# Four pairs of k-tiles instead of three by seven products in the FFNs of a decoder block, with a smaller descriptor ring and shared tiles

## The chip, the cores and the metric

The kernel runs on one core of a Trainium2 chip. The metric is the device time of one execution in microseconds (us); lower is better. Engines are named as in the profile: PE multiplies matrices, PEld loads its weights, DVE and ACT are the vector and scalar engines, POOL is GpSimd (it issues one kind of DMA here), SP issues nearly all other DMAs. A weight element is fp32 and is used as a rounded high half and a low half (the rest), both in a narrower fp32 type that PE takes.

## The reference, cut to what matters

One decoder block over 256 rows of width 2048, all in fp32:

```python
h = h + 0.5 * swiglu(rms_norm(h, ffn1_norm), ffn1_w_gu, ffn1_w_down)     # FFN1
h = h + hybrid_mixer(rms_norm(h, mix_norm), ...)                         # mixer
h = h + 0.5 * swiglu(rms_norm(h, ffn2_norm), ffn2_w_gu, ffn2_w_down)     # FFN2
gate = sigmoid(rms_norm(h, ple_norm) @ ple_w_gate)                       # last stage
h = h + gate * (p @ ple_w_proj)
out = rms_norm(h, final_norm)

def swiglu(x, w_gu, w_down):
    gate, up = split(x @ w_gu, 2)        # w_gu 2048 x 11264, w_down 5632 x 2048
    return (silu(gate) * up) @ w_down
```

## The kernel before, in words

**Products.** The weights stream from HBM in pairs of k-tiles (a tile is 128 rows; a pair is 128x1024 numbers, 512 KB, tile `raw`). ACT rounds a pair to `whi` (L70), DVE takes the rest `wlo` (L71), and PE does three matmuls for each product of 128x128 by 128x512: high by high, high by low, low by high. The next weights are asked for two ahead (`LEAD`); `raw` has four buffers, `whi` and `wlo` three. The input is split the same way (`nTh`/`nTl` for the normalised input, `hTh`/`hTl` for silu(gate)*up).

**Groups.** Each FFN is done in 17 groups, in three parts of 3, 4 and 4 gate/up blocks: a "gu" group is one 512-column block of gate and one of up over K = 2048 (eight pairs of k-tiles each), a "dn" group is two 512-column blocks of the down product over the part's K (six or eight pairs). After a part's gu groups come its two dn groups, so the order is gu0 to gu2, dn, dn, gu3 to gu6, dn, dn, gu7 to gu10, dn, dn.

**Seven products.** Of most groups the first `ns` pairs of both blocks don't go by plain products but as a 2x2 block product by seven products (Winograd's form of Strassen's): rows of the input in two halves of 128, columns in the two blocks, K in the two k-tiles of a pair. The weights' four quarters, raw and unsplit, are tiles R00, R01, R10 and R11 of 128 x (ns x 512) elements with one buffer each, loaded by SP (L269). Seven sums S0 to S6 are formed from them by `all_sums`: each is rounded by ACT (`shi`, L282) and its rest taken by DVE (`slo`, L283), two buffers each. R00 is the source of S0, S1, S2 and S5; it changes in between by two additions on DVE (L287), and after S2 by a DMA that adds a quarter read again from HBM (`add_loaded`, L291, issued from POOL). R01 is added to in the same way after S0. Each sum then feeds 3 x ns matmuls (L314 to L316), and at two of the seven ACT copies and DVE adds move partial results between the four PSUM banks (L321, L322). The matching sums of the input are made by the generator `halves`, two pairs at a time: an addition high + low (tile `tT`, L396), four additions and subtractions (tile `S`, L403), the rounding on ACT (`Sh`, L404), the rest on DVE (`Sl`, L405).

**The order of work.** The seven products of a group are carried out during the group ahead of it, between that group's plain pairs. `plan` writes this order: list `at` says after which plain pairs the sevenths stand, `loads` after which of them the R loads of the group after next are asked for. Weights, sums and loads go through one FIFO, `order`, drained by `next_weights`. Behind every plain pair `lanes.step()` advances generators with work on DVE, ACT and SP: lane 0 has a gu group's output (L426: times up, then the 32x32 transposes L165 and two DMAs through DRAM, then the split into `hTh`/`hTl`, L434 and L435) and the norms' transposes, lane 1 has `halves`. A scheduler of the framework then fixes each engine's instruction order. All queues are in order: what stands behind a waiting instruction waits too.

**The other stages.** The mixer between the FFNs is not touched. In the last stage (`fin`), for three column blocks, `embed` multiplies the embeddings p by `w_pp` (one pair), `accumulate` multiplies the normalised h by `w_pg` (eight pairs), and `gated` applies the sigmoid and updates h on DVE (L578 to L586).

Of the kernel before, what the change touches and what calls it, by code (L numbers as in the profile page):

```python
# [10 lines left out]
F32 = mybir.dt.float32  # L11
# [18 lines left out]
NS = 3  # L30
NS_DOWN = tuple(3 if i1 - i0 == 4 else 2 for i0, i1 in PARTS)
# [8 lines left out]
def block_kernel(ctx, tc, a, out):  # L40
# [156 lines left out]
    def norm_block(nT, which, j, tmp):  # L197

        if j < 3:
            lanes.add(0, norm_block_behind(nT, which, j, tmp))  # L200
            return
# [129 lines left out]
    def plan(n):  # L331
# [17 lines left out]
        made = []  # L349
        for i, group in enumerate(groups):  # L350
# [3 lines left out]
            at, loads = [], {}  # L354
            if follower is not None and follower.ns:
                first = 2 if group.ns else 8
                at = [first + j * (n_plain - 1 - first) // 7 for j in range(7)]
                if not group.ns:

                    loads.setdefault(max(at[0] - 5, 0), []).extend(follower.loads())  # L360
                if after is not None and after.ns:
                    for x, one in zip((5, 6, 7, 7), after.loads()):
                        loads.setdefault(at[x] if x < 7 else min(at[6] + 1, n_plain - 1), []).append(one)
# [16 lines left out]
    for nb in range(3):  # L380
        order += [("pair", a["w_pp"][nb])] + [("pair", a["w_pg"][nb][g]) for g in range(KD // 2)]
    order.append(("pair", a["w_pp"][3]))

    def halves(kind, his, los, ns, wait=0):
# [7 lines left out]
        for g0 in range(0, ns, 2):  # L392
# [3 lines left out]
            nc.vector.tensor_tensor(out=x, in0=hi[:, 0:2 * n].bitcast(F32).rearrange("p k x -> p (k x)"),  # L396
                                    in1=lo[:, 0:2 * n].bitcast(F32).rearrange("p k x -> p (k x)"), op=ALU.add)
            x = x.rearrange("p (g j t y) -> p g j t y", g=n, j=2, t=2)
            a11, a12, a21, a22 = (x[:, :, j, t, :] for t in range(2) for j in range(2))
            s = fp.tile([P, 4, 2, P], F32, tag="S", name="S")[:, :, 0:n]  # L400
            for o, y, z, op in ((0, a21, a22, ALU.subtract), (1, s[:, 0], a11, ALU.subtract),
                                (2, a21, a11, ALU.subtract), (3, s[:, 1], a12, ALU.add)):
                nc.vector.tensor_tensor(out=s[:, o], in0=y, in1=z, op=op)  # L403
            nc.scalar.copy(sh[:, :, g0:g0 + n], s)  # L404
            nc.vector.tensor_tensor(out=sl[:, :, g0:g0 + n], in0=s, in1=sh[:, :, g0:g0 + n], op=ALU.subtract)  # L405
            yield
# [9 lines left out]
        sides[kind] = side  # L416

    def ffn(n, nT, r, scale, next_norm, stat):
        xs = picker(*nT)
        late = callable(r)  # L420
        with tc.tile_pool(name="ffn", bufs=1) as fp:
# [24 lines left out]
            for group, todo in ffn_plan[n]:  # L446
# [11 lines left out]
                for kind, one in todo:  # L458
# [19 lines left out]
                    if dn:  # L478
# [7 lines left out]
                        if group.last:  # L486
                            norm_block(nxt, next_norm, nb, lambda: fp.tile([P, 2, 4, P], F32, tag="tT", name="tT"))
                            lanes.advance(0)
# [755 lines left out]
```

## Time and profile before

| what | value |
|---|---|
| median of 3 runs | 1964.15 us (1963.59 to 1965.22) |
| the profiled execution, and its span | 1965.08 us, 1963.4 us |
| granted PE clock, mean | 0.997 |
| busy PE, DVE, ACT (share of the span) | 99%, 78%, 59% |
| FFN1, mixer, FFN2, last stage (us from the span's start) | 0 to 702, 702 to 1165, 1165 to 1854, 1854 to 1963 |
| DMA queues, share of 16 engines' span | hardware 61.9%, software (POOL's) 13.5% |

In a row of instructions the columns are line, engine, operation, out<-in by tile names with shapes, count, then the busy sum in us and the mean of one in ns, and the idle time of the engine just ahead of them with what ended it. A row of waits reads: who waited for whom, us in total, times, the longest. A row of DMA issues has the count, the size of one and the median time from issue to landing. A timeline row is start, length, engine, line, operation, and in brackets how long the engine had been idle and for what.

### The profile page before, as it was taken

What the parts mean: (1) busy time and instruction counts of PE and PEld (TensorE: products, weight loads), DVE (VectorE), ACT (ScalarE), POOL (GpSimd) and SP (SyncE); (2) the same over time, 40 slices, a digit from 0 to 9 for tenths busy, and PEclk for the clock granted to TensorE, in tenths of its full rate; (3) what the DMA queues carried; (4) which work ended last, traced back from release to release, by engine and by line L of the source; (5) the groups of instructions that cost most, each with busy time, mean ns of one, the idle gap of its engine ahead of it and who ended that gap; (6) DMA issues with size and microseconds to landing.
All of it is one profiled execution on the core that took longest, in us unless ns stands there. A gap on an engine that the chain in (4) does not pass through costs nothing. (4 is left out here: it accounts for less than half of the span.)

```text
span 1963.4 us, 24730 instructions
## 1 busy us (share of the span) xinstructions
PE 1943.0 (99%) x8941; PEld 1606.3 (82%) x8941; DVE 1534.3 (78%) x1771; ACT 1151.2 (59%) x1401; POOL 83.3 (4%) x108
## 2 busy tenths in 40 slices
PE   9999999999999999999999999999999999999998
PEld 7887888888888888878878888888888888888887
DVE  6879878887888766794786678888889887798755
ACT  6655655565656557654545456565566555665554
POOL 0000000000000000000100000000000000000000
PEclk9999999999999999999999999999999999999999
DMA  9978887888888764555564788887888878887764
GB/s 298 301 238 253 268 263 244 264 257 247 265 274 242 224 215 159 179 178 195 175 200 149 250 284 245 255 266 248 252 262 265 289 231 242 256 275 243 235 208 146
DMA packets 166554, 468.28 MB, mean 239 GB/s; under 512 B 20640, under 2 KB 59552, under 8 KB 166304
## 3 DMA queue, kind: packets, MB, share of 16 engines
q1 hardware_dynamic: 156352, 418.57, 61.9%
q0 software_dynamic: 8928, 46.67, 13.5%
q10 hardware_dynamic: 1152, 1.47, 0.3%
q8 instruction: 70, 1.15, 0.2%
q14 instruction: 52, 0.43, 0.1%
HBM read 444.62 MB, written 22.02 MB: 238 GB/s over the span
## 5 line engine op out<-in xcount | busy, mean ns | idle before, releaser
L70 ACT CAST whi<-raw 128x1024 fp32r<-128x1024 f32 (+1 forms) x531 | 557.3, 1051 | 535.0 <-PE pj L107 110.9
L71 DVE TENSOR_TENSOR wlo<-raw,whi 128x1024 fp32r<-128x1024 f32 (+1 forms) x531 | 643.8, 1217 | 211.6 <-ACT whi L70 208.2
L283 DVE TENSOR_TENSOR slo<-R,shi 128x1536 fp32r<-128x1536 f32 (+1 forms) x217 | 365.8, 1687 | 129.0 <-ACT shi L282 127.3
L282 ACT CAST shi<-R 128x1536 fp32r<-128x1536 f32 (+1 forms) x217 | 309.7, 1429 | 170.0 <-PE g L316 47.2
L472 PE MATMUL g<-wlo,nTh 128*128 128x512 f32 x476 | 186.8, 392 | 0.5 <-DVE wlo L71 0.5
L471 PE MATMUL g<-whi,nTh 128*128 128x512 f32 x476 | 185.0, 390 | 2.2 <-ACT whi L70 2.2
L473 PE MATMUL g<-whi,nTl 128*128 128x512 f32 x476 | 186.2, 391 | 0.0
L472 PE MATMUL u<-wlo,nTh 128*128 128x512 f32 x476 | 185.3, 389 | 0.0
L471 PE MATMUL u<-whi,nTh 128*128 128x512 f32 x476 | 185.3, 389 | 0.0
L473 PE MATMUL u<-whi,nTl 128*128 128x512 f32 x476 | 185.3, 389 | 0.0
L105 PE MATMUL pj<-whi,nTh 128*128 128x512 f32 x448 | 179.7, 402 | 0.0
L106 PE MATMUL pj<-wlo,nTh 128*128 128x512 f32 x448 | 175.9, 393 | 2.2 <-DVE wlo L71 2.0
L472 PE MATMUL d<-wlo,hTh 128*128 128x512 f32 x448 | 174.6, 390 | 1.0 <-DVE wlo L71 1.0
L107 PE MATMUL pj<-whi,nTl 128*128 128x512 f32 x448 | 175.4, 391 | 0.0
L471 PE MATMUL d<-whi,hTh 128*128 128x512 f32 x448 | 174.5, 389 | 0.0
L473 PE MATMUL d<-whi,hTl 128*128 128x512 f32 x448 | 174.4, 389 | 0.0
L472 PEld LDWEIGHTS g<-wlo,nTh 128*128 128x128 f32 x476 | 89.8, 189 | 21.0 <-DVE wlo L71 2.4
L471 PEld LDWEIGHTS g<-whi,nTh 128*128 128x128 f32 x476 | 89.5, 188 | 21.3 <-ACT whi L70 2.8
L287 DVE TENSOR_TENSOR R<-R 128x1536 f32<-128x1536 f32 (+1 forms) x62 | 104.5, 1686 | 0.9
L473 PEld LDWEIGHTS g<-whi,nTl 128*128 128x128 f32 x476 | 89.8, 189 | 18.5
L473 PEld LDWEIGHTS u<-whi,nTl 128*128 128x128 f32 x476 | 89.4, 188 | 18.6
L471 PEld LDWEIGHTS u<-whi,nTh 128*128 128x128 f32 x476 | 89.4, 188 | 18.5
(304 smaller groups left out, 3221.5 us busy)
## 6 DMA issues: line engine op xcount, KB each, us to landing
raw<-in_w_gu SPq DMA_DIRECT2D x220, 512.0 KB, 5.6
raw<-in_w_down SPq DMA_DIRECT2D x112, 512.0 KB, 5.4
raw<-in_w_in SPq DMA_DIRECT2D x112, 512.0 KB, 3.4
R<-in_w_gu2q SPq DMA_DIRECT2D x40, 768.0 KB, 5.8
R<-in_w_gu1q SPq DMA_DIRECT2D x36, 768.0 KB, 6.1
scr<-tb SPq DMA_DIRECT2D x74, 256.0 KB, 4.8
raw<-in_w_out SPq DMA_DIRECT2D x32, 512.0 KB, 4.6
raw<-in_w_pg SPq DMA_DIRECT2D x32, 512.0 KB, 4.3
```

The costliest lines, as they stand in the source:

```text
L70: nc.scalar.copy(hi[:, j, :], raw[:, j, :])
L71: nc.vector.tensor_tensor(out=lo[:, j, :], in0=raw[:, j, :], in1=hi[:, j, :], op=ALU.subtract)
L105: nc.tensor.matmul(outs[t], xh[:, c], whi[:, j, :], start=st, stop=False)
L106: nc.tensor.matmul(outs[t], xh[:, c], wlo[:, j, :], start=False, stop=False)
L107: nc.tensor.matmul(outs[t], xl[:, c], whi[:, j, :], start=False, stop=sp)
L282: nc.scalar.copy(hi, w)
L283: nc.vector.tensor_tensor(out=lo, in0=w, in1=hi, op=ALU.subtract)
L287: nc.vector.tensor_tensor(out=self.raw[x], in0=self.raw[x], in1=self.raw[y], op=ALU.add)
L471: nc.tensor.matmul(out, xh[:, c], whi[:, j, :], start=st, stop=False, skip_group_check=True)
L472: nc.tensor.matmul(out, xh[:, c], wlo[:, j, :], start=False, stop=False, skip_group_check=True)
L473: nc.tensor.matmul(out, xl[:, c], whi[:, j, :], start=False, stop=sp, skip_group_check=True)
```

## The change

Of the groups that use seven products, all but the four dn groups of the first part and of each FFN's kind with six pairs now do four pairs that way (half of K), not three: 27 of 31 groups. Sums and quarters of these groups are 128x2048 instead of 128x1536 (1 MB instead of 768 KB a load), and two plain pairs per group fall away. `plan` puts the sevenths behind consecutive plain pairs, from the second pair on (from the third, where the follower is of the other kind; from the ninth in a group without sevenths of its own), instead of spreading them; the R loads of the group after next stand at the fifth, sixth and seventh seventh, and the fourth load at the start of the next group (`carried`).

The room for it comes from the ring of DMA descriptors in on-chip memory (`dynamic_dma_scratch_size`, 4096 instead of the default 16384) and from tiles that share a buffer: `S` of `halves` now uses the tag of `sil` (the silu(gate) tile), and half of the norms' transposed blocks do too, on lane 1. The split of the embeddings' input (`ph`, `pl`) stood ahead of FFN2 in a pool of its own; it is now a generator in the last stage, on lane 2. There the embed's pair also comes behind the gate's eight pairs, not ahead of them.

```diff
-NS = 3
-NS_DOWN = tuple(3 if i1 - i0 == 4 else 2 for i0, i1 in PARTS)
+NS = 4
+NS_DOWN = tuple(4 if i1 - i0 == 4 else 2 for i0, i1 in PARTS)
...
-    def norm_block(nT, which, j, tmp):
+    def norm_block(nT, which, j, tmp, lane=0):
 
         if j < 3:
-            lanes.add(0, norm_block_behind(nT, which, j, tmp))
+            lanes.add(lane, norm_block_behind(nT, which, j, tmp))
...
-        made = []
+        made, carried = [], []
...
-            at, loads = [], {}
+            at, loads, carried = [], {0: carried}, []
             if follower is not None and follower.ns:
-                first = 2 if group.ns else 8
-                at = [first + j * (n_plain - 1 - first) // 7 for j in range(7)]
+                first = 8 if not group.ns else 1 if group.kind == follower.kind else 2
+                at = [min(first + j, n_plain - 1) for j in range(7)]
                 if not group.ns:
 
                     loads.setdefault(max(at[0] - 5, 0), []).extend(follower.loads())
                 if after is not None and after.ns:
-                    for x, one in zip((5, 6, 7, 7), after.loads()):
-                        loads.setdefault(at[x] if x < 7 else min(at[6] + 1, n_plain - 1), []).append(one)
+                    *three, last = after.loads()
+                    for x, one in zip((4, 5, 6), three):
+                        loads.setdefault(at[x], []).append(one)
+                    carried = [last]
...
-        order += [("pair", a["w_pp"][nb])] + [("pair", a["w_pg"][nb][g]) for g in range(KD // 2)]
+        order += [("pair", a["w_pg"][nb][g]) for g in range(KD // 2)] + [("pair", a["w_pp"][nb])]
...
-            s = fp.tile([P, 4, 2, P], F32, tag="S", name="S")[:, :, 0:n]
+            s = fp.tile([P, 4, 2, P], F32, tag="sil", name="S")[:, :, 0:n]
...
-                            norm_block(nxt, next_norm, nb, lambda: fp.tile([P, 2, 4, P], F32, tag="tT", name="tT"))
-                            lanes.advance(0)
+                            norm_block(nxt, next_norm, nb, lambda x=("tT", "sil")[nb % 2]:
+                                       fp.tile([P, 2, 4, P], F32, tag=x, name="tT"), nb % 2)
+                            lanes.advance(nb % 2)
...
-    pp = ctx.enter_context(tc.tile_pool(name="pp", bufs=1))
-    pT = act.tile([P, 2, T], F32, tag="nat", name="pT", bufs=4)
-    nc.sync.dma_start(out=pT, in_=a["pT"])
-    ph = pp.tile([P, 2, T], F32R, tag="ph", name="ph")
-    pl = pp.tile([P, 2, T], F32R, tag="pl", name="pl")
-    nc.scalar.copy(ph, pT)
-    nc.vector.tensor_tensor(out=pl, in0=pT, in1=ph, op=ALU.subtract)
...
+        ph = fp.tile([P, 2, T], F32R, tag="ph", name="ph")
+        pl = fp.tile([P, 2, T], F32R, tag="pl", name="pl")
+
+        def split_p():
+            pT = act.tile([P, 2, T], F32, tag="nat", name="pT", bufs=4)
+            nc.sync.dma_start(out=pT, in_=a["pT"])
+            for _ in range(3):
+                yield
+            nc.scalar.copy(ph, pT)
+            nc.vector.tensor_tensor(out=pl, in0=pT, in1=ph, op=ALU.subtract)
+
+        lanes.add(2, split_p())
...
         for nb in range(3):
-            e = embed(nb)
             gt = [mm_ps("gt") for _ in range(2)]
             accumulate(gt, xs, KD)
+            e = embed(nb)
...
-    nc = _bacc.Bacc("TRN2", target_bir_lowering=False, num_devices=1)
+    nc = _bacc.Bacc("TRN2", target_bir_lowering=False, num_devices=1, dynamic_dma_scratch_size=4096)
```

**DVE in the last gu group of the second part.** From the low half of S1 to that of S2 (tiles: `slo` of a sum, `wlo` of a plain pair, `R` an addition to a quarter, `S`, `Sl` and `tT` the halves of the following dn group's input), DVE's order before was:

```order
L283 TENSOR_TENSOR slo<-R,shi 128x1536
L71 TENSOR_TENSOR wlo<-raw,whi 128x1024
L287 TENSOR_TENSOR R<-R 128x1536
L403 TENSOR_TENSOR S<-tT 128x128 x2
L403 TENSOR_TENSOR S<-S,tT 128x128
L71 TENSOR_TENSOR wlo<-raw,whi 128x1024
L403 TENSOR_TENSOR S<-S,tT 128x128
L71 TENSOR_TENSOR wlo<-raw,whi 128x1024
L405 TENSOR_TENSOR Sl<-S,Sh 128x4x128
L283 TENSOR_TENSOR slo<-R,shi 128x1536
```

and in the changed kernel, for the same stretch and the four rows behind it (L409, L416 and L418 are the lines of `halves` now):

```order
L283 TENSOR_TENSOR slo<-R,shi 128x2048
L416 TENSOR_TENSOR S<-S,tT 128x256
L287 TENSOR_TENSOR R<-R 128x2048
L418 TENSOR_TENSOR Sl<-S,Sh 128x4x256
L409 TENSOR_TENSOR tT<-hTh,hTl 128x1024
L71 TENSOR_TENSOR wlo<-raw,whi 128x1024
L416 TENSOR_TENSOR S<-tT 128x256 x2
L416 TENSOR_TENSOR S<-S,tT 128x256
L283 TENSOR_TENSOR slo<-R,shi 128x2048
L416 TENSOR_TENSOR S<-S,tT 128x256
L71 TENSOR_TENSOR wlo<-raw,whi 128x1024 x2
L418 TENSOR_TENSOR Sl<-S,Sh 128x4x256
```

The last part of the first pass of the halves, which stood ahead of this stretch, is in it now, with the addition `tT` of the second; the second pass is twice as wide and its end has moved behind S2.

**ACT in the last stage.** From the weights ahead of the first sigmoid (`sg`, L582, now L590) to those behind it, ACT's order before was:

```order
L70 CAST whi<-raw 128x1024 x5
L582 ACT_TABLE_LOAD
L582 ACTIVATE sg<-gt,rstd_15319 128x512 x2
L70 CAST whi<-raw 128x1024 x2
L218 ACTIVATE junk,stat<-h 128x512 x2
L70 CAST whi<-raw 128x1024 x7
```

and now, with the input's rounding `ph` in it:

```order
L70 CAST whi<-raw 128x1024 x3
L578 CAST ph<-pT 128x512
L70 CAST whi<-raw 128x1024 x4
L590 ACT_TABLE_LOAD
L590 ACTIVATE sg<-gt,rstd_14911 128x512
L70 CAST whi<-raw 128x1024
L590 ACTIVATE sg<-gt,rstd_14911 128x512
L70 CAST whi<-raw 128x1024
L218 ACTIVATE junk,stat<-h 128x512
L70 CAST whi<-raw 128x1024
```

The two sigmoids stood together ahead of the next weights; now a weight pair stands between them.

More of the change, by code (lines that the diff above doesn't have):

```diff
@@ L391, in halves, with side @@
         sl = fp.tile([P, 4, NS, P], F32R, tag="Sl", name="Sl")
+        def side(i, g):
+            if i in (0, 4, 5):
+                k, t = 2 * (g % 2) + (i > 0), i // 5
+                c = slice(t * P, (t + 1) * P)
+                return his[g // 2][:, k, c], los[g // 2][:, k, c]
+            x = {1: 0, 2: 1, 3: 2, 6: 3}[i]
+            return sh[:, x, g, :], sl[:, x, g, :]
+        sides[kind] = side
         for g0 in range(0, ns, 2):
@@ L406, in halves @@
             yield
-        def side(i, g):
-            if i in (0, 4, 5):
-                k, t = 2 * (g % 2) + (i > 0), i // 5
-                c = slice(t * P, (t + 1) * P)
-                return his[g // 2][:, k, c], los[g // 2][:, k, c]
-            x = {1: 0, 2: 1, 3: 2, 6: 3}[i]
-            return sh[:, x, g, :], sl[:, x, g, :]
-        sides[kind] = side
     def ffn(n, nT, r, scale, next_norm, stat):
```

## The prediction

> **What bounds the kernel now.** I read the page's head, then PE's own waits, then the stages one by one, and last the transfers.
>
> ```profile
> span 1963.4 us, 24730 instructions
> PE 1943.0 (99%) x8941; PEld 1606.3 (82%) x8941; DVE 1534.3 (78%) x1771; ACT 1151.2 (59%) x1401; POOL 83.3 (4%) x108
> PE g L471 <- ACT whi L70: 2.2, 2, 1.6
> PE d L472 <- DVE wlo L71: 1.0, 1, 1.0
> PE u L314 <- ACT Sh L404: 0.8, 1, 0.8
> 467.40:508.90 41.50, 41.50 (x185) 34.39 (x184) 31.29 (x26) 24.22 (x23) 1.74 (x2) 1.00 0.81 241
> 300.10:341.60 41.50, 41.50 (x184) 34.38 (x184) 34.71 (x34) 24.09 (x25) 0.87 (x1) 1.00 0.86 266
> 341.60:383.10 41.50, 41.50 (x184) 34.29 (x183) 36.46 (x37) 25.10 (x27) 1.75 (x2) 1.00 0.82 266
> 425.90:467.40 41.50, 41.50 (x185) 34.39 (x184) 34.36 (x34) 23.49 (x22) 1.75 (x2) 1.00 0.78 242
> ```
>
> PE is busy for 99% of the span, and all its waits in both FFNs come to a few us. The windows are four FFN groups (columns: length, then PE, PEld, DVE, ACT, POOL busy, the clock, the DMA share, GB/s): PE fills each, DVE between 31.3 and 36.5 us of 41.5. So a matmul less is time less, as long as DVE and the transfers keep up. A group of gate and up columns followed by its like is ten plain pairs of 12 matmuls and seven products of 9: 183 in 41.50 us, 226.8 ns each.
>
> **Matmuls: the gain.** The order of instructions has 648 plain matmuls less (L471 to L473, 216 each) and 567 more in products (L314 to L316, 189 each): 81 less. 81 x 0.2268 = **18.4 us**. In that group it is 180 instead of 183, 40.8 us instead of 41.5.
>
> **What DVE and ACT pay.** 54 weight pairs are not split any more, but sums, differences and additions of 27 groups become a third wider.
>
> ```profile
> L71 DVE TENSOR_TENSOR wlo<-raw,whi 128x1024 fp32r<-128x1024 f32 x529 | 642.4, 1219 | 211.1 <-ACT whi L70 207.8 <-DMA raw<-in_w_down 1.5
> L283 DVE TENSOR_TENSOR slo<-R,shi 128x1536 fp32r<-128x1536 f32 x189 | 331.7, 1756 | 125.4 <-ACT shi L282 124.9
> L283 DVE TENSOR_TENSOR slo<-R,shi 128x1024 fp32r<-128x1024 f32 x28 | 34.1, 1222 | 3.7 <-ACT shi L282 2.4
> L287 DVE TENSOR_TENSOR R<-R 128x1536 f32<-128x1536 f32 x54 | 94.7, 1755 | 0.8
> L405 DVE TENSOR_TENSOR Sl<-S,Sh 128x1024 fp32r<-128x1024 f32 x12 | 14.6, 1221 | 1.2 <-ACT Sh L404 1.2
> L405 DVE TENSOR_TENSOR Sl<-S,Sh 128x512 fp32r<-128x512 f32 x10 | 6.9, 685 | 0.0
> L403 DVE TENSOR_TENSOR S<-S,tT 128x256 f32<-128x256 f32 x24 | 10.1, 420 | 0.1
> L403 DVE TENSOR_TENSOR S<-S,tT 128x128 f32<-128x128 f32 x20 | 5.7, 287 | 0.0
> L396 DVE TENSOR_TENSOR tT<-hTh,hTl 128x1024 f32<-128x1024 f32 x6 | 7.3, 1224 | 0.2
> L282 ACT CAST shi<-R 128x1536 fp32r<-128x1536 f32 x189 | 280.4, 1484 | 163.7 <-PE g L316 45.2 <-DVE R L287 42.3 <-PE u L316 20.2
> L282 ACT CAST shi<-R 128x1024 fp32r<-128x1024 f32 x28 | 29.3, 1055 | 6.2 <-PE d L316 4.3 <-PE g L316 2.0
> ```
>
> 512 elements more cost DVE 1756 - 1222 = 534 ns, so a 128x2048 is some 2290; on ACT 1484 - 1055 = 429, so 1913. Per group DVE gets 9 x 0.534 = 4.8 us more and loses 2 x 1.22 = 2.4. In a plain neighbour of its kind that is covered: 34.71 + 2.4 = 37.1 of 40.8. It is not covered in the last gate/up group before a down group (341.6 to 383.1, four such in the program, two per FFN). There the second pass of the down input's halves grows from one pair to two (685 to 1221 in L405, four times 287 to 420 in L403: 1.1 us), and, by the order, that pass's L396 (1.2) and the first pass's four of L403 (1.7) now stand in this group, not in the one ahead: 36.46 + 2.4 + 1.1 + 1.2 + 1.7 = 42.9 us of work in 40.8. DVE falls 2.1 us behind there.
>
> What is late then is the third sum, S2. These rows have its low half before and the matmul that takes it:
>
> ```profile
> 338.58 1.76 DVE L283 TENSOR_TENSOR slo<-R,shi 128x1536 fp32r<-128x1536 f32 x1 [2.49 <-ACT shi L282]
> 356.52 1.76 DVE L283 TENSOR_TENSOR slo<-R,shi 128x1536 fp32r<-128x1536 f32 x1 [0.33 <-ACT shi L282]
> 359.32 0.39 PE L314 MATMUL d<-shi,Sh 128*128 128x512 f32 x1
> ```
>
> From S0's low half to the end of S2's DVE needed 19.7 us, and S2 was ready 1.0 us before PE wanted it (358.28 against 359.32). Now the same stretch is 2.5 us longer by its instructions' durations: wide sums, a full pass of halves, one pair less. ACT is held too: its two Silu instructions (L440, now L443) take the tile that S shares with them, so they wait for the second Sl, and the cast of S3 stands behind them. Against that, PE's order now puts matmuls of later plain pairs between those of S1 and S2. Between nothing (all covered) and 4.6 us (2.1 of DVE's lag, 2.5 of the longer stretch) per place, I take 1.8, the 2.5 less most of the row's 1.0 us of spare time: **+7 us** for four. In the down groups before gate/up (425.9 to 467.4) the same additions give 34.36 + 2.4 + 1.1 = 37.9 of 40.8: nothing, up to 2 us each.
>
> **The raw quarters' loop.** One buffer, R(0,0), is loaded, summed three times, gets an accumulating DMA after S2, is read for S5, and is loaded again. It must close once per group.
>
> ```profile
> 461.61 1.76 DVE L283 TENSOR_TENSOR slo<-R,shi 128x1536 fp32r<-128x1536 f32 x1 [1.24 <-ACT shi L282]
> 470.79 1.75 DVE L287 TENSOR_TENSOR R<-R 128x1536 f32<-128x1536 f32 x1
> 479.29 1.76 DVE L283 TENSOR_TENSOR slo<-R,shi 128x1536 fp32r<-128x1536 f32 x1 [1.24 <-ACT shi L282]
> 481.34 0.87 POOL L291 DMA_DIRECT2D R<-in_w_gu1q  x1 [14.78 <-DVE slo L283]
> 494.53 1.76 DVE L283 TENSOR_TENSOR slo<-R,shi 128x1536 fp32r<-128x1536 f32 x1 [0.56 <-ACT shi L282]
> 496.32 0.33 SPq L269 DMA_DIRECT2D R<-in_w_gu1q  x1
> 503.09 1.76 DVE L283 TENSOR_TENSOR slo<-R,shi 128x1536 fp32r<-128x1536 f32 x1 [1.24 <-ACT shi L282]
> R<-in_w_gu1q SPq DMA_DIRECT2D x36, 768.0 KB, 6.1
> R<-in_w_down10q SPq DMA_DIRECT2D x8, 512.0 KB, 4.4
> R<-in_w_gu1q POOLq DMA_DIRECT2D x18, 768.0 KB, 8.5
> R<-in_w_down10q POOLq DMA_DIRECT2D x4, 512.0 KB, 6.1
> ```
>
> S0 at 461.61, the add, S2 at 479.29, the accumulating DMA at 481.34, S5 at 494.53, the load at 496.32, S0 again at 503.09: 41.5 us, one group. But S2 comes 6.8 us after the add that it needs (472.5), since it waits for one of two sum buffers that PE still reads; that time is spare. By the rows 256 KB more cost a load 1.7 us (7.8 in all) and an accumulation 2.4 (10.9). With the new order PE takes a sum every 24 matmuls, 5.44 us: S0's buffer is free 8.2 us into the group, S2 is ready 1.91 + 2.29 later at 12.4, the accumulation has landed at 12.4 + 0.9 + 10.9 = 24.2, S5 (its buffer is free at 24.5) is ready at 28.7 and wanted at 32.6; the load lands at 36.5, the next S0 is ready at 40.7 and wanted at 46.2. The loop closes with 4 us to spare: **nothing**, at most 1 us a group.
>
> By the Trainium skill's "DMA: Bandwidth & Descriptors" (section "Anatomy of one DMA — SWDGE (gpsimd) path") such a DMA takes 2.0 us and its bytes over 436 GB/s, so that 256 KB more would cost 0.6 us as an estimate, not 2.4; the rows disagree with that slope, and by it the loop would have 2 us more to spare. Its "SBUF — State Buffer" (section "SBUF: two separate sides") speaks against the change: while VectorE holds the port pair in a two-port mode, GpSimd can't write the descriptors; the issue at 481.34 took 0.87 us with DVE at 75%, so no such hold is seen.
>
> **Starts, last stage, the rest.** The first seven-product group of each FFN has its four loads sent in one burst while the plain group runs: 1.05 MB more.
>
> ```profile
> GB/s 298 301 238 253 268 263 244 264 257 247 265 274 242 224 215 159 179 178 195 175 200 149 250 284 245 255 266 248 252 262 265 289 231 242 256 275 243 235 208 146
> 1884.43 0.61 PE L105 MATMUL gt<-whi,nTh 128*128 128x512 f32 x2
> 1885.45 0.50 PE L106 MATMUL gt<-wlo,nTh 128*128 128x512 f32 x1 [0.41 <-DVE wlo L71]
> 1853.60:1963.40 109.80, 99.94 (x489) 84.28 (x487) 63.45 (x81) 54.98 (x78) 1.81 (x3) 0.97 0.56 183
> ```
>
> At the fastest slice's 301 GB/s that is 3.5 us at most, or nothing if the prefetch covers it; I take 2 for each: **+4 us**. In the last stage DVE's gated chain held back a weight and PE stood 0.41 us; with the embed after the gate's matmuls the chain is covered: **-0.4**. The embeddings' input is split there by one ACT and one DVE instruction; DVE is busy 63.45 of 109.8, which hides it (some 0.7 us on DVE if it didn't). The smaller ring holds the descriptors of two accumulations a group, issued at least 15 us apart, each landing in about 11: nothing. Fewer, larger loads move the same bytes: nothing.
>
> **Sum.** 1965.08 (the profiled execution; span 1963.4) - 18.4 - 0.4 + 7 + 4 = 1957.3. The median of the runs lies 0.9 below the profiled one: **1956 us**.
>
> **Rivals.** (1) *Nothing is late*: PE keeps its pace everywhere, 1964.15 - 18.8 = 1945. For it: PE waited hardly anywhere before. Against it: 42.9 us of DVE work in 40.8. (2) *The gain is eaten*: stalls of 15 to 23 us in all, 1960 to 1968. (3) *DVE becomes the bound around each change of kind*: its lag is not made good in the down group that follows (its input's transposes wait behind it), 4 x 4.6 at the gate/up side, 4 x 2 at the down side and 4 at the starts: 30 us, 1964.15 - 18.8 + 30 = 1975, slower. It decides from some 23 us of stalls in all. For it: the 2.1 us of lag and ACT's shared tile; against it: by the windows the groups beside have 40.8 - 37.1 = 3.7 us of DVE free, or 7.1 after the down groups. (4) *The loop of R(0,0) becomes the bound*: accumulations of over 15 us (10.9 and the 4 to spare), whether through traffic or the smaller ring; each us beyond costs one in each of some 20 groups, so at 17 us 1956 + 40 = 1996. Against it: 8.5 us now.
>
> **How the numbers follow.** Forecast (1948 to 1960) 0.47, (1) 0.18, (2) 0.11, (3) 0.16, (4) 0.08. A difference under 0.2%, 3.9 us here, can't be told from none: faster is below 1960.2, 0.65; within, 0.11; slower, above 1968.1, 0.24. The likeliest's own range is 1948 to 1960; the range 1942 to 1978 takes in (1), (2) and most of (3).
>
> **What would show it.** Right: gate/up groups of 40.8 us with PE full, 128x2048 sums of 2.29 us, PE's new waits only at the ends of the gate/up runs and at the two starts, on DVE's low halves, 1 MB accumulations landing in 10 to 12 us, no gap in the last stage. Wrong: PE's waits on S5 or S0 in every group (the loop), DVE over 40 us in every group, or waits on plain weights behind the larger loads.

## The result, and the profile after

| | before | after |
|---|---|---|
| median of the runs | 1963.87 us (1961.9 to 1965.22) | 2035.74 us (2032.86 to 2036.79) |
| span of the profiled execution | 1963.4 us | 2035.1 us |
| ratio | | 1.036, 95% interval 1.034 to 1.038 |

The change made the kernel 3.6% slower, where I had forecast 1956 us and a range up to 1978. The page of the changed kernel, and below it the two transfer queues of the kernel before:

```profile
span 2035.1 us, 24266 instructions
PE 1960.0 (96%) x8860; PEld 1597.2 (78%) x8860; DVE 1605.2 (79%) x1717; ACT 1168.9 (57%) x1347; POOL 83.9 (4%) x108
q1 hardware_dynamic: 149344, 418.57, 58.5%
q0 software_dynamic: 8928, 60.82, 16.5%
```

```profile
q1 hardware_dynamic: 156352, 418.57, 61.9%
q0 software_dynamic: 8928, 46.67, 13.5%
```

The 81 matmuls are gone (8941 to 8860), yet PE is busy 17 us longer. Two sums separate what happened. At the old pace PE would be busy 1943.0 - 18.4 = 1924.6 us; it is busy 1960.0, so 35.4 us went into matmuls that took longer. It stands idle 2035.1 - 1960.0 = 75.1 us, against 20.4 before: 54.7 more. Together -18.4 + 35.4 + 54.7 = 71.7 us, the difference of the spans. By stage, FFN1 lost 26.8 us, the mixer 6.4, FFN2 36.8 and the last stage 1.7.

The waits of the changed kernel (who waited for whom: us in total, times, the longest):

```profile
PE g L315 <- DVE slo L283: 22.3, 15, 2.9
PE g L314 <- ACT shi L282: 11.3, 8, 3.0
ACT shi L282 <- DVE R L287: 84.9, 41, 4.8
ACT hTh L437 <- DMA tT<-scr: 74.8, 16, 9.2
ACT shi L282 <- DMA R<-in_w_gu2q: 30.1, 14, 3.6
ACT shi L282 <- DMA R<-in_w_gu1q: 28.2, 12, 4.4
```

PE waits for sums; behind the sums stands ACT, which waits for DVE's additions, for the raw quarters and, in 16 places, for the transposed FFN output to come back from DRAM. The waits for the additions and for the quarters are mostly there too in a kernel below that loses next to nothing (75.4 us for L287, and 36.3 for the quarters of the last two rows together). Put to the sum whose cast or low half ended it, PE waited 42.6 us for sums: 31.1 of them for S4, 5.2 for S3, 4.1 for S2, and 1.1 each for S0 and S5. Before, ACT's wait for the transposes was 3.3 us in all:

```profile
L434 ACT CAST hTh<-tT 128x512 fp32r<-128x512 f32 x44 | 25.0, 617 | 3.3 <-DMA tT<-scr 3.3
```

**One group closely.** The third gate/up group of the second part took 41.5 us before and 47.9 now. First its transposes in the kernel before, from the scaled output (`sil`) to the rounding `hTh`:

```profile
301.70 1.40 DVE L426 SCALAR_TENSOR_TENSOR sil<-u,rstd,sil 128x512 f32<-128x512 f32 x2
304.89 0.92 SPq L169 DMA_DIRECT2D scr<-tb  x2
311.83 2.54 SPq L179 DMA_DIRECT2D tT<-scr  x4
318.06 1.14 ACT L434 CAST hTh<-tT 128x512 fp32r<-128x512 f32 x2 [1.27 <-DMA tT<-scr]
```

and the same in the changed kernel, with the fifth sum S4 behind it:

```profile
308.84 2.28 DVE L287 TENSOR_TENSOR R<-R 128x2048 f32<-128x2048 f32 x1
311.04 0.75 DVE L429 SCALAR_TENSOR_TENSOR sil<-u,rstd,sil 128x512 f32<-128x512 f32 x1
313.56 3.12 SPq L169 DMA_DIRECT2D scr<-tb  x2
322.45 2.54 SPq L179 DMA_DIRECT2D tT<-scr  x4
333.92 1.14 ACT L437 CAST hTh<-tT 128x512 fp32r<-128x512 f32 x2 [8.53 <-DMA tT<-scr]
334.97 1.89 ACT L282 CAST shi<-R 128x2048 fp32r<-128x2048 f32 x1
336.89 2.29 DVE L283 TENSOR_TENSOR slo<-R,shi 128x2048 fp32r<-128x2048 f32 x1 [1.02 <-ACT shi L282]
336.91 0.49 PE L314 MATMUL g<-shi,nTh 128*128 128x512 f32 x1 [2.31 <-ACT shi L282]
339.24 0.80 PE L315 MATMUL g<-slo,nTh 128*128 128x512 f32 x1 [1.83 <-DVE slo L283]
339.83 0.63 PE L316 MATMUL g<-shi,nTl 128*128 128x512 f32 x1
```

A wide addition now separates the two `sil` instructions, and the last transfer from DRAM lands after 333, 8.5 us after ACT was ready for it. ACT's queue is in order: S4's rounding stands behind `hTh`, S4's low half behind that, and PE behind both. The windows of this stretch show what PE's two waits cost beside themselves (columns: length, then PE, PEld, DVE, ACT, POOL busy, granted clock, DMA share, GB/s):

```profile
307.20:355.10 47.90, 43.76 (x182) 35.47 (x182) 38.00 (x30) 25.32 (x23) 1.75 (x2) 0.93 0.81 253
337.40:344.20 6.80, 4.97 (x13) 3.94 (x13) 6.80 (x7) 4.70 (x5) 0.00 (x0) 0.50 0.79 296
344.20:355.10 10.90, 10.90 (x50) 9.00 (x49) 8.54 (x6) 5.94 (x4) 0.00 (x0) 1.00 0.92 357
```

The waits are 2.31 + 1.83 = 4.1 us. From 337.4 to 344.2 the granted clock is 0.50, and a matmul takes 0.43 us of PE's time there, start to start, instead of 0.23. So the group lost 4.1 us idle, and 43.76 - 40.8 = 3.0 us in which PE is busy longer: waits of this length cost nearly twice themselves. Over the whole trace 91 matmuls started 0.36 to 0.5 us after the one ahead of them, against 24 before; that is 13 of the 35.4 us. Some 10 more are the ends of matmuls ahead of a wait, which count as busy, and the rest is spread over matmuls a little slower.

The clock fell at 337.4, behind the first wait and before the second. In this trace it fell in or right behind each of the six waits of 2 us or more (2.07 to 3.10 us), and three waits of 1.8 us that stood alone left it as it was; in the kernel with both accumulations on DVE, below, two of 2.31 and 2.35 us did too. The Trainium skill's "TensorE: Matmul & The Clock Gate" (section "HAM oscillation — how this bites in real kernels") gives as its rule that PE should have no idle gaps of more than about 3.4 us. Here shorter ones were enough, so for this kernel the measured 2 us count.

### The profile page after: what moved, and what is told of

It is laid out like the page before. It is cut to its first block, busy times and chain, and to the rows that moved or that the text cites. A ratio compares the mean times of both kernels' runs of the same rounds, so it can differ in the third digit from the quotient of the medians.

```text
span 2035.1 us, 24266 instructions
## 1 busy us (share of the span) xinstructions
PE 1960.0 (96%) x8860; PEld 1597.2 (78%) x8860; DVE 1605.2 (79%) x1717; ACT 1168.9 (57%) x1347; POOL 83.9 (4%) x108
## 3 DMA queue, kind: packets, MB, share of 16 engines
q1 hardware_dynamic: 149344, 418.57, 58.5%
q0 software_dynamic: 8928, 60.82, 16.5%
## 5 line engine op out<-in xcount | busy, mean ns | idle before, releaser
L70 ACT CAST whi<-raw 128x1024 fp32r<-128x1024 f32 (+1 forms) x477 | 497.8, 1048 | 380.8 <-PE pj L107 111.3
L71 DVE TENSOR_TENSOR wlo<-raw,whi 128x1024 fp32r<-128x1024 f32 (+1 forms) x477 | 576.3, 1215 | 166.7 <-ACT whi L70 161.6
L283 DVE TENSOR_TENSOR slo<-R,shi 128x2048 fp32r<-128x2048 f32 (+1 forms) x217 | 466.0, 2148 | 110.7 <-ACT shi L282 109.0
L282 ACT CAST shi<-R 128x2048 fp32r<-128x2048 f32 (+1 forms) x217 | 390.7, 1802 | 259.9 <-DVE R L287 84.9
L287 DVE TENSOR_TENSOR R<-R 128x2048 f32<-128x2048 f32 (+1 forms) x62 | 132.8, 2142 | 0.4
L315 PE MATMUL g<-slo,nTh 128*128 128x512 f32 x228 | 94.7, 415 | 18.3 <-DVE slo L283 18.3
L314 PE MATMUL g<-shi,nTh 128*128 128x512 f32 x228 | 93.7, 411 | 11.3 <-ACT shi L282 11.3
L106 PEld LDWEIGHTS pj<-wlo,nTh 128*128 128x128 f32 x448 | 84.5, 189 | 23.6 <-DVE wlo L71 7.7
L107 PEld LDWEIGHTS pj<-whi,nTl 128*128 128x128 f32 x448 | 84.3, 188 | 17.4
L105 PEld LDWEIGHTS pj<-whi,nTh 128*128 128x128 f32 x448 | 84.4, 189 | 16.9 <-ACT whi L70 0.2
```

The lines of the kernel that those rows point to most:

```text
L70: nc.scalar.copy(hi[:, j, :], raw[:, j, :])
L71: nc.vector.tensor_tensor(out=lo[:, j, :], in0=raw[:, j, :], in1=hi[:, j, :], op=ALU.subtract)
L105: nc.tensor.matmul(outs[t], xh[:, c], whi[:, j, :], start=st, stop=False)
L106: nc.tensor.matmul(outs[t], xh[:, c], wlo[:, j, :], start=False, stop=False)
L107: nc.tensor.matmul(outs[t], xl[:, c], whi[:, j, :], start=False, stop=sp)
L282: nc.scalar.copy(hi, w)
```

## The experiments

Medians are compared with the kernel before, run beside each. "Needs" is 180 matmuls at 226.8 ns, 40.8 us a group.

### Is it the transposes' wait alone?

Where a group and its follower are gate/up groups, the rounding `hTh` and the low half `hTl` of the output wait two steps longer and are issued behind the newest sum's.

```diff
+                for _ in range(late):
+                    yield
+                with ExitStack() as after_sum:
+                  if late:
+                    for ins in last_sum:
+                        after_sum.enter_context(tc.issue_after(ins))
                   for t in range(2):   # hTh, hTl
...
```

> The changed kernel, but ACT's rounding of the transposed gate/up product (hTh, L437) and DVE's rest (hTl, L438) are queued behind the newest traced sum's cast and difference (two yields later, issue order only), except for the last block of a part. Theory A: in the gate/up groups ACT stands up to 9.2 us for the transposes' DMA (74.8 us in 16 waits), and the cast of S4 stands behind it; then the time falls by 55 to 75 us, from 2035.7 to 1960 to 1980, gate/up groups come to 41 to 42 us, and S4 is not late any more. Rival B (the loop of the raw quarters: ACT's waits for additions to R 84.9 us and for R's loads 58 us): moving the casts leaves the loop as it is, over 2020. Rival C (DVE's work): over 2015, DVE fuller than 95% in these groups.

Measured: 2022.04 us, ratio 1.029 (1.025 to 1.032). The wait for `tT` is gone, and only 14 of the 72 us with it, as these waits of that kernel show:

```profile
ACT shi L282 <- DVE R L286: 97.7, 49, 4.8
ACT whi L70 <- DMA raw<-in_w_gu: 53.5, 13, 7.4
ACT hTh L442 <- DMA tT<-scr: 1.2, 2, 1.0
```

ACT now waits 53.5 us for the raw pairs (6.6 before the edit). The wait moved to the next late transfer, so the theory that this one place is the cause fell.

### Without the accumulations

`add_loaded` is left out altogether: S3 and S5, which read the quarters that it changes, miss an addend, and nothing else changes (S2, S4 and S6, called wrong below, are as before).

```diff
-                    add_loaded((0, 1), (1, 1))
-                elif i == 2:
-                    add_loaded((0, 0), (1, 0))
```

> The changed kernel without the two accumulating DMAs of each seven-product group (its sums S2 to S6 are then wrong; the load, casts, additions on DVE and all matmuls stay). Theory A, if the transposes' DMAs are late because 1 MB accumulations share the engines with them: tT's landing falls from a median of 5.0 us to 3.5, ACT's wait for it from 74.8 us to under 25, and the time to under 1985. Theory A, if they are late because DVE issues the transposes later: ACT's wait stays over 50 us and the time over 2010. Rival B: the loop is 10 us shorter per group, waits on R go, under 1975.

Measured: 1966.75 us, ratio 1.001 (0.999 to 1.003): 69 us less than the changed kernel. The same kinds of group as above, and the mixer:

```profile
305.30:346.10 40.80, 40.80 (x181) 33.78 (x180) 36.66 (x29) 25.85 (x23) 0.00 (x0) 1.00 0.68 233
388.00:430.00 42.00, 41.52 (x181) 33.47 (x180) 37.43 (x31) 25.53 (x22) 0.00 (x0) 1.00 0.71 248
595.40:637.30 41.90, 41.60 (x182) 33.53 (x181) 39.94 (x40) 25.66 (x24) 0.00 (x0) 1.00 0.54 191
700.40:1167.90 467.50, 459.81 (x2362) 378.06 (x2362) 325.29 (x571) 260.88 (x436) 25.15 (x34) 1.00 0.59 190
tT<-scr SPq DMA_DIRECT2D x124, 128.0 KB, 3.3
raw<-in_w_gu SPq DMA_DIRECT2D x176, 512.0 KB, 5.0
```

The plain group is 40.8 us with PE full, as the matmul count asks. The transposes land in 3.3 us and the raw pairs in 5.0; in the changed kernel it is

```profile
tT<-scr SPq DMA_DIRECT2D x124, 128.0 KB, 5.0
raw<-in_w_gu SPq DMA_DIRECT2D x176, 512.0 KB, 6.5
```

So nearly the whole loss needs the accumulating DMAs. What is left is instructive too: with none of them the change still gains nothing. The FFNs gain 1.6 and 3.3 us instead of 18.4, since the groups at a change of kind stay over 40.8 by about 1 us each and the start of FFN1 loses 2.6 more than before, and the mixer and the last stage lose 4.6 and 1.2.

### Which part of the change needs them

Three kernels: seven products over three pairs again, in the new places; four pairs in the old places; and three pairs in the old places, so that only tiles, ring and last stage are changed.

```diff
-NS = 4                 # first and third kernel
+NS = 3
-                first = 8 if not group.ns else 1 if group.kind == follower.kind else 2
-                at = [min(first + j, n_plain - 1) for j in range(7)]
+                first = 2 if group.ns else 8        # second and third kernel
+                at = [first + j * (n_plain - 1 - first) // 7 for j in range(7)]
...                    # the R loads likewise at their old places
```

> The changed kernel with three pairs instead of four (as before), everything else of the change kept: the new places of the sevenths and loads, shared tiles, small ring, the input's split in the last stage. If the width is what costs: 1960 to 1970, as before. If the new places cost by themselves: over 1980. Theory A says that the wait for tT comes with the wide sums (DVE and the accumulations), so under 25 us of it here.

> The changed kernel with the old formula for the places of the sevenths and of the loads, four pairs kept. If the new places are what makes the transposes late: 1955 to 1985. If it is the width: as slow as the change, 2015 to 2060, with ACT's wait for tT over 50 us. Rival B expects 2010 to 2060 too, but with ACT waiting for R and not for tT.

> The changed kernel with three pairs and with the old places of sevenths and loads: only the shared tiles, the small ring and the last stage's edits are left of the change. With three pairs and the new places the time was 1984.1. If the 20 us there came from the new places: 1960 to 1966. If from the shared tiles or the ring: 1975 to 1990. The last stage alone was forecast at 0.4 us less.

Measured: 1984.09 (1.009; 1.007 to 1.011), 2048.03 (1.041; 1.038 to 1.044) and 1975.0 (1.005; 1.003 to 1.006). From the kernel before, then: side edits +11, new places +9, the fourth pair +52; with the old places the fourth pair costs 73. With four pairs the new places are not at fault: they give back 12 us. In the first kernel the wait for `tT` is there at 34.2 us, against 8.2 in the third: sums that stand closer together bring some of it by themselves.

### The side edits one by one

Shared tiles and lanes alone, the ring alone, and the last stage's edits alone, each on the kernel before.

```diff
-            s = fp.tile([P, 4, 2, P], F32, tag="S", name="S")[:, :, 0:n]
+            s = fp.tile([P, 4, 2, P], F32, tag="sil", name="S")[:, :, 0:n]
-                            lanes.advance(0)
+                            lanes.advance(nb % 2)
```

> The kernel before with the shared tiles alone: S uses the tag of sil, half of the norms' blocks too, on lane 1. The shared tiles, the small ring and the last stage's edits together took 10.9 us more. If the tiles are it (the norm's blocks at the end of an FFN wait for each other, and the mixer starts later): 1972 to 1976. If not: 1963 to 1966.

> The kernel before with the descriptor ring of 4096 bytes alone. If the ring holds back the accumulations, their landing (8.4 and 8.5 us) or POOL's issue (0.87 us) grows, and the time is 1967 or more. If it does nothing, as I forecast: 1962 to 1966.

> The kernel before with the edits of the last stage alone (the embeddings' input split there, the embed's pair behind the gate's eight); tiles, ring, places and widths as before. With the shared tiles alone costing 15.7 us and all side edits together 10.9, these edits should gain up to 5 us if the costs add: 1959 to 1961. If the difference came from how the shared tiles fell out in the schedule, it gains the 0.4 us that PE stood in the last stage, or nothing: 1963 to 1965.

Measured: 1979.91 (1.008; 1.006 to 1.011), 1966.62 (1.000; 0.999 to 1.002), 1964.65 (1.000; 0.999 to 1.001). Ring and last stage cost nothing and gain nothing. The shared tiles cost it all, and not in the FFNs: the mixer takes 9.3 us more than the 462.9 of before, the last stage 3.0. Kernel with shared tiles alone:

```profile
702.40:1174.60 472.20, 460.73 (x2362) 379.48 (x2361) 324.45 (x568) 261.14 (x436) 24.79 (x34) 1.00 0.59 190
PE abT L740 <- issue: 3.6, 1, 3.6
```

PE waits 3.6 us ahead of the mixer's `abT` product, 0.2 before (L739), where the norm's transposed blocks now share lane 1 and a buffer with the sums of the halves; the granted clock is at 0.5 for 3.4 us behind that wait. Which of the two shared uses costs was not taken apart. I had expected a gain of up to 5 us from the last stage as the difference between all side edits and the tiles; there is none, and the intervals of those two runs touch.

### What of an accumulation costs

Other ways to get the sum, each a change of the one line in `add_loaded`:

```diff
-                nc.gpsimd.dma_start(out=self.raw[x], in_=self.quarters[y[1]][y[0]], accum_op=ALU.add)
+                nc.gpsimd.dma_start(out=away, in_=self.quarters[y[1]][y[0]])       # copies elsewhere
+                nc.gpsimd.dma_start(out=away, in_=self.raw[x])                     # the quarter copied out
+                nc.gpsimd.dma_start(out=self.raw[x], in_=self.raw[y], accum_op=ALU.add)   # from on-chip memory
+                nc.gpsimd.tensor_tensor(out=self.raw[x], in0=self.raw[x], in1=self.raw[y], op=ALU.add)   # on POOL
+                add(x, y)                                                          # on DVE
```

> The changed kernel with each accumulating DMA replaced by a plain DMA of the same quarter from the same queue to a scratch in DRAM that nobody reads (sums S2 to S6 are then wrong): the traffic stays, at least in part, the wait for it goes. Without the accumulations at all the time was 1966.75. Theory T (traffic: what POOL's queue moves makes the loads and the transposes land late): tT's landing stays near 5.0 us and raw's near 6.5, time over 2000. Theory L (the wait: S3 and S5 stand until the accumulation has landed): 1965 to 1975.

Measured: 2147.02 us, ratio 1.092 (1.090 to 1.095), but it answers another question than I asked. With nothing to wait for, the copies ran ahead, all issued in the first 227 us; there PE stood for 130 of 207 us:

```profile
53.00:260.00 207.00, 76.67 (x270) 58.42 (x270) 50.45 (x54) 43.28 (x58) 24.19 (x49) 0.66 0.95 324
q0 software_dynamic: 2880, 60.82, 8.2%
```

Traffic that no sum waits for can hold PE up, but the rate isn't that of the changed kernel. What it does give is a price: the same 60.82 MB as a plain copy took 8.2% of the engines in 2147.0 us, 2.89 us of all 16 engines per MB, the same as the hardware queue's loads of before (61.9% of 1963.4 us for 418.57 MB: 2.90). As accumulations they took 16.5% of 2035.1 us: 5.52 per MB, 1.9 times as much.

> The changed kernel with each accumulating DMA replaced by a DMA of the raw quarter from on-chip memory to a scratch in DRAM (S2 to S6 are then wrong): traffic of 1 MB at about the accumulations' places, once per place, and no sum waits for it; only the quarter's next load does. Theory T (traffic slows the loads and the transposes): tT's landing over 4 us, raw's over 5.7, time 1985 or more. Theory L (the wait of S3 and S5 for the accumulation itself): 1964 to 1975, as without accumulations (1966.8).

Measured: 2036.22 us, ratio 1.037 (1.032 to 1.041): no sum waits for a copy there, only the next load of that quarter, and the time is that of the changed kernel. But the waits lie elsewhere (ACT waits 135 us for DVE's additions and 84 for the quarters), since the loads behind the copies now take 7.6 us. The transposes landed in 3.6 us and the raw pairs in 5.6, and PE waited for S0 to S2, never for S4. So the kernel lost as much by another wait, and it doesn't decide. It does show that the number of packets is not what makes an accumulation dear: as many packets took less than half the time.

```profile
q0 software_dynamic: 8928, 60.82, 7.7%
```

> The changed kernel with the accumulating DMAs reading the quarter that is on the chip already instead of reading it from HBM once more (same values). Theory T, if the engines' time per byte is what counts: landing 8 to 10 us as before, 2020 to 2040. Theory T, if HBM's part is what counts: landing 6 to 8 us, 1985 to 2010. Theory L: it falls with the landing time, 1 us of it is worth some 20.

Measured: 2023.16 us, ratio 1.030 (1.027 to 1.032).

```profile
q0 software_dynamic: 8928, 60.82, 16.4%
R<-R POOLq DMA_DIRECT2D x54, 1024.0 KB, 8.5
```

Without reading HBM the accumulations' packets take as long (16.4%) and land little sooner. The second read of the weights is not the price; the accumulation is.

> The changed kernel with each accumulating DMA replaced by an addition on POOL from the quarter that lies in on-chip memory already (same values): no traffic, but a wait for POOL. Theory T: as without accumulations, 1962 to 1975, if the addition takes under 10 us (no row shows it; DVE's of this size takes 2.28) and DVE is not slowed by POOL. Theory L: still 1990 or more if the addition takes as long as the DMA did (9 us). If POOL and DVE hinder each other, L283 and L287 of 128x2048 take over 2.4 us in the mean and the time is over 1985.

Measured: 2159.01 us, ratio 1.099 (1.097 to 1.101).

```profile
L71 DVE TENSOR_TENSOR wlo<-raw,whi 128x1024 fp32r<-128x1024 f32 x475 | 686.1, 1451 | 153.0 <-ACT whi L70 149.3 <-DMA tT<-scr 1.5 <-DMA raw<-in_w_down 1.5
L283 DVE TENSOR_TENSOR slo<-R,shi 128x2048 fp32r<-128x2048 f32 x189 | 512.6, 2715 | 88.2 <-ACT shi L282 86.9
L291 POOL TENSOR_TENSOR R<-R 128x2048 f32<-128x2048 f32 x54 | 298.5, 5527 | 993.1 <-DVE R L287 597.2 <-issue 274.9 <-ACT part L321 56.5
```

An addition takes POOL 5.5 us, and DVE's own instructions grow from 1217 to 1451 and from 2286 to 2715 ns in the mean: the two engines hold each other up. Few instructions bear it all. Of the 189 wide low halves, the 160 that ran clear of POOL's additions took 2.28 us, and the 29 that ran beside one took 5.11 in the mean and up to 6.73. The Trainium skill's "SBUF — State Buffer" (section "SBUF: two separate sides") says that a DVE instruction with two inputs from on-chip memory and a GpSimd instruction that reads that memory shut each other out of a shared pair of ports; these times agree.

> The changed kernel with the two accumulating DMAs as two more additions on DVE (same values): 54 x 2.28 + 8 x 1.22 = 133 us more work for DVE, no traffic, no wait for POOL. If traffic alone was the trouble and DVE has room: 1965 to 1985. DVE works 82 to 84% in the gate/up groups of the changed kernel, so 4.6 us more per group is 93 to 95%; where it is at 100% already (the groups ahead of a change of kind), 4.6 us more are lost each: 12 such groups, up to 50 us, 2010. I expect 1985.

Measured: 2006.83 us, ratio 1.021 (1.019 to 1.023). Six of the eight plain groups take 40.8 us again, but DVE is full where the kind changes (the last gate/up group of the third part):

```profile
606.90:651.90 45.00, 42.53 (x181) 33.40 (x180) 45.00 (x43) 25.65 (x24) 0.00 (x0) 1.00 0.57 192
```

### One accumulation of two, and the waits against the traffic

What stayed open was whether a sum's wait for its own accumulation costs, or the DMA engines' time. Each of the two accumulations was put on DVE alone (first: R01 += R11, wanted for S3; second: R00 += R10, wanted for S5), and then both, but only where a group is of the kind of the one ahead of it.

```diff
-                    add_loaded((0, 1), (1, 1))      # first kernel
+                    add((0, 1), (1, 1))
-                    add_loaded((0, 0), (1, 0))      # second kernel
+                    add((0, 0), (1, 0))
+                if self.alike:                      # third kernel, in add_loaded
+                    return add(x, y)
```

> The changed kernel with the first of a group's two loaded additions (R01 += R11, after S0) on DVE, the second (R00 += R10, after S2) still an accumulating DMA. The two differ in how tightly they are waited for: R01 is wanted next for S3, R00 for S5. *Theory W (what costs is that one sum waits for its accumulation)*: one of the two kernels, this one or the one with the second on DVE, gets nearly all of the 69 us back but DVE's own 40 (that version with both on DVE: 2006.8), the other next to none. *Theory T (what costs is the DMA engines' time that an accumulation takes, by which the raw quarters, the raw pairs and the transposes land late)*: each of the two gets about half of it; with one accumulation a group the transposes land in 4 us (5.0 with two, 3.3 with none), the raw pairs in 5.7 (6.5 and 5.0), and gate/up groups followed by their like come near 42 us. With half of DVE's price at the changes of kind, T gives 1995 to 2015 for each.

> The mirror: R00 += R10 (after S2) on DVE, R01 += R11 (after S0) still an accumulating DMA. Theory T: as the other one, 1995 to 2015, the two within 10 us of each other, the transposes' landing near 4 us. Theory W: the two are 20 us or more apart, and the slower one keeps the waits of ACT's rounding on DMA R that the changed kernel has (58 us).

> The changed kernel with both loaded additions on DVE where the group during which they are made and the group that uses them are of the same kind (there DVE had room: 40.8 us a group with both on DVE), and as accumulating DMAs at the changes of kind (there DVE had none). Theory T: between the version without accumulations (1966.8) and 1985, since what the accumulations cost where they are left falls with their number; 1975. It beats the changed kernel, and does not beat the kernel before. If the accumulations cost by something that lasts through the whole program whatever their number, it stays above 1990.

Measured: 2025.89 (1.032; 1.029 to 1.035), 2010.21 (1.025; 1.022 to 1.028) and 1988.42 (1.012; 1.010 to 1.014). Totals mix what accumulations cost with what DVE pays, so here are mean lengths of groups in the profiled executions, in us, each group counted by the matmuls that it needs in PE's order. "Plain" are the eight gate/up groups with gate/up groups on both sides, "last gu" the four before a down group of the second and third parts, "first dn" the four down groups behind those.

| kernel | accumulations a group | plain | last gu | first dn | median |
|---|---|---|---|---|---|
| before (needs 41.5) | 2 of 768 KB | 41.5 | 41.5 | 41.8 | 1964 |
| changed | 2 | 45.7 | 44.4 | 44.8 | 2035.7 |
| `hTh` behind the sums | 2 | 42.4 | 44.0 | 46.7 | 2022.0 |
| first on DVE | 1 | 42.5 | 47.9 | 44.5 | 2025.9 |
| second on DVE | 1 | 42.1 | 44.0 | 44.3 | 2010.2 |
| DVE where alike | 0 or 2 | 41.2 | 43.2 | 41.6 | 1988.4 |
| both on DVE | 0 | 41.0 | 45.1 | 41.9 | 2006.8 |
| none at all | 0 | 40.8 | 41.9 | 41.8 | 1966.8 |

In the plain groups, where DVE has room, it makes little difference which accumulation goes: 42.5 and 42.1, from 45.7. Landing times fall in both. With the first on DVE, and then with the second:

```profile
tT<-scr SPq DMA_DIRECT2D x124, 128.0 KB, 3.7
raw<-in_w_gu SPq DMA_DIRECT2D x176, 512.0 KB, 6.0
```

```profile
tT<-scr SPq DMA_DIRECT2D x124, 128.0 KB, 3.1
raw<-in_w_gu SPq DMA_DIRECT2D x176, 512.0 KB, 5.5
```

That speaks for the engines' time and against one sum's wait. So does where PE stood in the changed kernel: the sums whose quarter an accumulation had just changed, S3 and S5, cost it 6.3 of the 42.6 us, and ACT waited 16.7 us for accumulations against 77.6 for the quarters' loads. Such a wait is not always small, though: with four pairs in the old places S5 alone cost PE 19.8 us. The two medians are 15.7 us apart, more than the 10 that theory T allowed and less than the 20 of theory W. The profiled executions, of which the table tells, are further apart (2038.1 and 2002.2 us); of these 36 us the last gate/up groups make 16, four times 3.9, where the first addition on DVE stands ahead of sums that are late already. My 1995 to 2015 for each held for one of them only, and for the mixed kernel I was 13 us too low: beside the version without accumulations it loses 1.3 us in each last gate/up group, about 2 in the second down group of each FFN's second part, and 0.4 in each plain group. It is the fastest form with four pairs that leaves nothing out, and still 1.2% slower than the kernel before.

## Why the prediction was wrong

- **The step that failed: "Fewer, larger loads move the same bytes: nothing", with "nothing, at most 1 us a group" for the loop of R(0,0).** The loads do move the same bytes (418.57 MB), but the accumulations read more (46.67 to 60.82 MB), and I priced them by one DMA's landing alone. Their packets take the engines 1.9 times as long per MB as a load's. The kernel before had the rows for it: a plain group used 0.86 x 41.5 = 35.7 us of all engines; two accumulations of 0.786 MB at 13.5% x 1963.4 / 46.67 = 5.68 us per MB are 8.9 of those; a third wider is 3.0 more. 38.7 us of a 40.8 us group is 95%. The changed group measured 0.81 x 47.9 = 38.8. Taking the accumulations away gave 69 us; the term was written down as nothing. The 95% is worked out afterwards and is no limit that a run shows.
- **The loop itself** is not what bound: 1 MB accumulations landed faster than my 10.9 us, and rival 4 (over 15) did not happen; PE's waits for S5 and S0, by which I had said it would show, are 1.1 us each in the whole program. In the changed kernel:

```profile
R<-in_w_gu2q POOLq DMA_DIRECT2D x20, 1024.0 KB, 9.3
R<-in_w_gu1q POOLq DMA_DIRECT2D x18, 1024.0 KB, 8.9
```

  That is 0.9 and 0.4 us more than 768 KB took (8.4 and 8.5). I had taken 2.4 from the smaller transfers of the down groups; the 0.6 estimated from the Trainium skill's "DMA: Bandwidth & Descriptors" (section "Anatomy of one DMA — SWDGE (gpsimd) path") was nearer. Both are the time of one transfer, and neither tells what it takes from the others.
- **The transposes are in none of my steps.** I didn't name ACT's `hTh` ahead of S4 as something that can wait for a DMA, though its 1.27 us stood in the trace of before.
- **"Each us beyond costs one"** (rival 4), and every stall in my sum at face value: too low. Beside the 54.7 us more of idle PE stand 35.4 in which it is busy longer, 13 of these in matmuls at about half the pace.
- **Four last gate/up groups at 1.8 us, and the starts at 2 each: +11.** Without accumulations the FFNs fall short of the 18.4 us by 13.5, at these places and at the down groups, which I had priced at "nothing, up to 2 us each". Roughly right in kind, spread differently: DVE's work in a last gate/up group, which I put at 42.9 us, is 39.9 there, and such a group loses 1.1 us and not 1.8.
- **Shared tiles at nothing but ACT's wait in the last group**: the mixer and the last stage lose 12.3 us in the kernel with them alone, and 8.1 in the changed kernel; I named no cover for the norm's blocks on lane 1. The last stage's -0.4 cannot be told from nothing in its own run.
- **Right:** 81 matmuls and 40.8 us a plain group (shown without accumulations), the ring at nothing, the 128x2048 durations to 4 ns:

```profile
L283 DVE TENSOR_TENSOR slo<-R,shi 128x2048 fp32r<-128x2048 f32 x189 | 431.9, 2286 | 105.4 <-ACT shi L282 104.0
L282 ACT CAST shi<-R 128x2048 fp32r<-128x2048 f32 x189 | 361.2, 1913 | 249.7 <-DVE R L287 84.9 <-DMA R<-in_w_gu2q 30.1 <-DMA R<-in_w_gu1q 28.2
```

**What stays open.** That the loss goes with the accumulations is shown, and in the plain groups that it matters little which of the two is there; through which transfer it acts in which group is shown for the transposes only (14 us), and what the waits for the accumulations themselves cost was not taken apart from it. The traffic alone, at the changed kernel's rate and with nothing waiting for it, was not had: in both kernels meant for it the waits moved. Nor is a limit of the DMA share found: the kernel before ran at 0.86 without loss, one accumulation a group at 0.70 and 0.74 (in two such groups) with a mean loss of 1.7 and 1.3 us. That its sums are wider and stand closer together may be why; it wasn't tried.

## What to carry to other kernels

Cost a wider transfer by the engines' time that its queue takes per MB, added to what the group uses already and divided by the group's new, shorter length, and not by one transfer's landing: the share rises from both sides when a change shortens the work and widens the DMAs. That is a warning and no limit, since the share from which it costs was not found. Where an in-order queue carries a step that waits for a DMA round trip, list what stands behind it before calling the DMAs free. And count waits of PE of 2 us and more nearly twice, since the granted clock can fall behind them.

## What the runs showed of the hardware

- The packets of accumulating DMAs took the 16 engines 5.5 us per MB, those of a plain copy or load 2.6 to 2.9; reading the source on chip instead of from HBM changed next to nothing (16.4% against 16.5%).
- In the changed kernel each of the six waits of PE of 2.07 to 3.10 us brought the granted clock to 0.5 for 3.4 or 6.8 us; a wait of 2.31 us was enough, though in another kernel one of 2.35 was not.
- An addition of 128x2048 on POOL took 5527 ns in the mean. DVE's low halves of that width took 2.28 us clear of such additions and 5.11 beside them (29 of 189). DVE's additions L287 kept their 2.28 us, and none of them ran beside one of POOL's.
